# Two token chunks projected from raw activations, and the step sizes ahead of the last values

## The chip, the cores and the metric

The kernel runs on one core of a Trainium2 chip. The metric is the device time of one execution in microseconds. A core has five engines that matter here: TensorE (matrix products into PSUM banks), VectorE, ScalarE and GpSimd (elementwise work), and SyncE, which with ScalarE issues the DMAs. Each engine takes its instructions in a fixed order.

## The reference

One decoder layer on 1024 tokens of 1024 channels, with 16 learned meta tokens in front (1040 tokens in all). What matters for the change is the beginning: a root-mean-square norm, a projection, and of its parts the stick-breaking attention's q, k and v and the SSM's raw step sizes.

```python
h = jnp.concatenate([pad, meta_tokens, x], axis=1)
hn = rmsnorm(h, mix_norm_g)            # x * rsqrt(mean(x*x) + 1e-6) * g, per token
proj = hn @ w_in
sb_q, sb_k, sb_v, ssm_z, ssm_xbc, ssm_dt, c_q, c_kv, k_r = jnp.split(proj, split_at, axis=-1)
o_sb  = stick_breaking_attention(sb_q, sb_k, sb_v, valid)     # 8 heads of 64
dt = jax.nn.softplus(ssm_dt + dt_bias) * valid                # 16 heads
dA = dt * -exp(a_log); Acs = cumsum(dA within blocks of 128)  # used by the SSD stage later
...                                    # SSD, latent attention, output projection, SwiGLU, final norm
```

The norm's factor 1/rms is one number per token, so a projection can be made from `x * g` and multiplied by the token's factor afterwards.

## The kernel before

Channels lie on partitions and tokens along the free axis. Every fp32 operand is split into a high and a low fp32r part, and each product is three matmuls (high x high, low x high, high x low) that add into one PSUM bank. `dense_fm` makes one such product for a chunk of tokens: 8 slices of channels x 3 = 24 matmuls. The bank comes from `dpool`, which has two (`d_ps`), and is free again when its evacuation function has read it. `HH` and `HL` (`hnh`, `hnl` in the profile, one tile for each of 8 channel slices) hold the high and low parts of the activations.

The tokens come in three chunks (`CH_ALL`): chunk 0 of 272, chunks 1 and 2 of 384 columns. The first stage makes, for each chunk, the keys (`w_k`) and queries (`w_q`) of the first pair of heads and the values (`w_v`) of half the heads, the latter in three blocks of up to 128 tokens, 24 matmuls of 256 columns each.

- Chunk 0 goes *raw*: `first_operands(0)` splits `x * g`, and the evacuations multiply by the token factor. `k_evac` and `q_evac` do it with `over_rms` (one VectorE product into `scaled`), `sb_values` by ScalarE's `scale`. Later `normalise(0, row)` overwrites `HH` and `HL` of chunk 0 for the rest of the kernel.
- Chunks 1 and 2 are normalised before they are projected. `chunk_rstd` squares x on ScalarE, adds the eight slices up on VectorE (`acc`), sums over channels by a matmul with ones (`ssum`), takes the power -1/2 on GpSimd (`rc`), spreads the factor over partitions by three matmuls (`rrow`) and copies it out (`row`). `normalise` multiplies x by gain and row on VectorE (in place in `xT`), casts the high part on ScalarE and subtracts the low part on VectorE, for chunk 0 mostly on GpSimd.

After that come the values' loads (`load_value_steps`, through DRAM tensor `s_vsb`; `vlast` and `V` are what the attention reads), then `step_sizes`: a projection with 96 columns (`w_dt`), transposes into `dtt`, a softplus by polynomial in some 20 small VectorE instructions, a running sum by one matmul (`acum`, copied to `AT`), its transposes (`acst`), and a split of that sum into three bf16 rows (`A3`, through slices of the buffers `raws[2]` and `raws[3]`, 18 VectorE instructions). Then the attention of four pairs of heads begins. Score products (`sc_ps`), a sigmoid on ScalarE and a scan on VectorE (`cm`), transposes (`ptm`, `ptg`) and weighted values (`pv`) follow each other; the projections of the next pair and the convolution units (`conv_unit`) are put between them.

The order on each engine is set by a scheduler that places the instructions by its own time line as it builds the program; `tc.high_priority` moves evacuations and statistics forward. Tiles come from pools with a fixed number of buffers, and a tile that reuses a buffer waits for the last reader of the one before.

Of the kernel before, what the change touches and what calls it, by code (L numbers as in the profile page):

```python
# [11 lines left out]
F32 = mybir.dt.float32  # L12
# [8 lines left out]
D = 1024  # L21
KT = D // 128
# [37 lines left out]
def tile_hybrid_block(ctx: ExitStack, tc: tile.TileContext, a: dict):  # L60
# [5 lines left out]
    def last_on(engine):  # L66
        return next(i for i in reversed(nc.cur_bb.bb.instructions) if i.engine == engine)
# [71 lines left out]
    def dense_fm(dpool, w, nkt, m, mov, chunks, evac):  # L139
        hi, lo = w  # L140
        for c0, n in chunks:
            ps = dpool.tile([128, 512], F32, tag="d", name="d_ps")
            for kt in range(nkt):
                mh, ml = mov(kt, c0, n)
                wh = hi[:, kt * m : (kt + 1) * m]
                wl = lo[:, kt * m : (kt + 1) * m]
                pe.matmul(ps[:m, :n], wh, mh, start=(kt == 0), stop=False)  # L147
                pe.matmul(ps[:m, :n], wl, mh, start=False, stop=False)  # L148
                pe.matmul(ps[:m, :n], wh, ml, start=False, stop=(kt == nkt - 1))  # L149
            with tc.high_priority(offset=1000):  # L150
                evac(ps, c0, n)

    def token_rstd(cols, ps, squares, blocks, width, bufs=1):


        for e, (t0, w) in enumerate(blocks):
            for i, sq in enumerate(squares):
                pe.matmul(
                    ps[:w, e : e + 1], sq[:, t0 : t0 + w], ones[:, 0:1], start=(i == 0), stop=(i == len(squares) - 1)
                )  # L160
        nb = len(blocks)
        r = cols.tile([128, nb], F32, tag=f"rc{nb}", bufs=bufs, name="rc")
        e0 = 0
        if blocks[0][1] < 128:
            w = blocks[0][1]
            dve.memset(r[:, 0:1], 1.0)
            dve.tensor_scalar(r[:w, 0:1], ps[:w, 0:1], 1.0 / width, EPS, ALU.mult, ALU.add)
            e0 = 1
        dve.tensor_scalar(r[:, e0:nb], ps[:, e0:nb], 1.0 / width, EPS, ALU.mult, ALU.add)
        pool.tensor_tensor(r, r, mhalf[:, :nb], op=ALU.pow)  # L170
        return r
# [24 lines left out]
    def fill_tile(tag, name):  # L196
        return fl.tile([128, 388 if tag == "craw" else 384], F32, tag=tag, name=name)
# [44 lines left out]
    def chunk_rstd(i):  # L242
        c0, n = CH_ALL[i]
        blocks = [(t0 - c0, w) for t0, w in BLOCKS[3 * i : 3 * i + 3]]
        acc = fill_tile("cacc", "acc")[:, :n]
        for k in range(KT):
            x = xT[:, k, c0 : c0 + n]
            sq = acc if k == 0 else sqs[k % 2][:, 512 * (k // 2 % 2) :][:, :n]
            act.activation(sq, x, AF.Square)
            if k > 0:  # L250
                dve.tensor_tensor(acc, acc, sq, op=ALU.add)
        ssum = ps0.tile([128, 4], F32, tag="ssum", name="ssum")
        with tc.high_priority(offset=200):
            r = token_rstd(p0, ssum, [acc], blocks, D, bufs=3)
            rrow = ps0.tile([128, 512], F32, tag="rrow", bufs=1, name="rrow")
            spread(rrow, r, blocks, 0)
            row = fill_tile("craw", "row")
            act.copy(row[:, :n], rrow[:, :n])
        return r, row

    def normalise(i, row):
        c0, n = CH_ALL[i]
        c = slice(c0, c0 + n)
        for k in range(KT):
            hn = xT[:, k, c]
            dve.scalar_tensor_tensor(hn, hn, gmix[:, k : k + 1], row[:, :n], ALU.mult, ALU.mult)
            act.copy(HH[k][:, c], hn)
            eng = pool if i == 0 and k not in (2, 5, 7) else dve
            eng.tensor_tensor(HL[k][:, c], hn, f32(HH[k][:, c]), op=ALU.subtract)
# [338 lines left out]
        return (Q, K, KS), k_evac, q_evac  # L608


    proj, k_evac, q_evac = sb_project(0)

    def first_pair(name):
# [7 lines left out]
    stats = [chunk_rstd(0)]  # L621
# [17 lines left out]
    sp.dma_start(acol, a["a_log"].partition_broadcast(128))  # L639
    for i, (q0, qn) in enumerate(((0, 256), (256, 384), (640, 384))):  # L640
        c0, n = CH_ALL[i]
        if i < 2:
            r1, row1 = chunk_rstd(i + 1)
            normalise(i + 1, row1)
        if i == 0:
            r, row = stats[0]
            dense_fm(dpool, w_k, KT, 128, hn_mov, [(c0, n)], lambda ps, t0, m: k_evac(ps, t0, m, row[:, :m]))
            t1 = META + q0 - c0
            dense_fm(dpool, w_q, KT, 128, hn_real, [(q0, qn)], lambda ps, t0, m: q_evac(ps, t0, m, row[:, t1 : t1 + m]))
            sb_values(0, w_v, range(3), r, ps0)  # L650
        else:
            dense_fm(dpool, w_k, KT, 128, hn_mov, [(c0, n)], k_evac)
            dense_fm(dpool, w_q, KT, 128, hn_real, [(q0, qn)], q_evac)
            sb_values(0, w_v, range(3 * i, 3 * i + 3), None, ps0)
    normalise(0, row)
    p0_st.close()

    with ctx_sb as st:
# [32 lines left out]
                    weighted_values(tp, pvp, sbb, j, rows, values[0], h, [x[p, 64 * h : 64 * (h + 1)] for x in (s_osbh, s_osbl)], pms[j % 2], values[1])  # L691

        values = load_value_steps(sbv, sbb, 0)
        step_sizes()
        convs = [8, 9, 10, 11, 0, 1, 2, 3, 4, 5, 6, 7]
        for p in range(4):
            sb_attend(p, proj, values)
# [1051 lines left out]
```

## Time and profile before

| | |
|---|---|
| median of 3 runs | 1794.79 us (1790.23 to 1795.47) |
| the profiled execution | 1792.69 us, its span 1791.0 us |
| mean granted TensorE clock | 0.978 |
| TensorE busy | 1714.3 us (96%), 9801 matmuls |
| VectorE busy | 1129.1 us (63%) |
| ScalarE busy | 842.9 us (47%) |
| GpSimd busy | 718.0 us (40%) |

The busy share is a mean over stages. The profile's slices show TensorE at nine tenths or more in nearly all of the span, and lower in the first 5%; a wait shows in brackets behind an instruction of the time line, with the engine and the tile that ended it. Line numbers are those of the kernel before.

### The profile page before, as it was taken

How to read it: one execution, taken by the hardware profiler on the slowest of the kernel's cores; microseconds unless marked ns; L12 is line 12 of the kernel's file. 1: busy time of each engine (PE TensorE's matmuls, PEld its weight loads, DVE VectorE, ACT ScalarE, POOL GpSimd, SP SyncE). 2: the span in 40 equal slices, each digit the busy share in tenths (PEclk: the TensorE clock that was granted, in tenths of full speed). 3: DMA queues.
4: the chain of work that ended last, by engine and by line, in shares of the span. 5: the costliest groups of instructions: out<-in, count | busy, mean ns of one | idle time of the engine just before them, and what ended most of it. 6: DMA issues, size and time to landing. Idle time of an engine off the chain costs nothing. (4 is left out here: it accounts for less than half of the span.)

```text
span 1791.0 us, 26537 instructions
## 1 busy us (share of the span) xinstructions
PE 1714.3 (96%) x9801; PEld 1505.6 (84%) x9801; DVE 1129.1 (63%) x1727; ACT 842.9 (47%) x1789; POOL 718.0 (40%) x503
## 2 busy tenths in 40 slices
PE   5969999999999998999999999999999999999998
PEld 5959998999988778998888887778888888878887
DVE  7476755777554564455675645887566666678654
ACT  6355555555566664677453433532222223244332
POOL 4232434434456556555321245554545555300002
PEclk8989999999999999999999998999999999999999
DMA  4221223222263455345531334122332322899702
GB/s 159 57 56 39 82 76 90 65 59 78 76 175 106 158 178 171 112 124 171 191 95 42 101 123 145 43 94 76 112 107 100 111 95 88 300 376 376 262 1 95
DMA packets 145639, 222.35 MB, mean 124 GB/s; under 512 B 24722, under 2 KB 84148, under 8 KB 145508
## 3 DMA queue, kind: packets, MB, share of 16 engines
q1 hardware_dynamic: 126112, 205.09, 35.2%
q10 hardware_dynamic: 19396, 15.56, 2.9%
q8 instruction: 77, 1.26, 0.3%
q14 instruction: 54, 0.44, 0.1%
HBM read 157.56 MB, written 63.04 MB: 123 GB/s over the span
## 5 line engine op out<-in xcount | busy, mean ns | idle before, releaser
L147 PE MATMUL d_ps<-hnh,whi 128*128 128x384 f32 (+6 forms) x744 | 247.7, 333 | 3.2 <-DVE KS L599 2.1
L149 PE MATMUL d_ps<-hnl,whi 128*128 128x384 f32 (+6 forms) x744 | 246.6, 331 | 0.0
L148 PE MATMUL d_ps<-hnh,wlo 128*128 128x384 f32 (+6 forms) x744 | 245.7, 330 | 0.0
L136 POOL TENSOR_TENSOR wlo<-wraw,whi 128x1024 fp32r<-128x1024 f32 (+1 forms) x57 | 138.6, 2432 | 191.8 <-ACT whi L134 190.4
L147 PEld LDWEIGHTS d_ps<-hnh,whi 128*128 128x128 f32 (+1 forms) x744 | 140.5, 189 | 8.0 <-DVE KS L599 2.5
L149 PEld LDWEIGHTS d_ps<-hnl,whi 128*128 128x128 f32 (+1 forms) x744 | 140.6, 189 | 3.3 <-issue 1.0
L148 PEld LDWEIGHTS d_ps<-hnh,wlo 128*128 128x128 f32 (+1 forms) x744 | 140.7, 189 | 2.3 <-issue 0.2
L1257 PE MATMUL b_ps<-T,wl 128*128 128x512 f32 x352 | 138.8, 394 | 1.3 <-POOL wl L1088 1.3
L1258 PE MATMUL b_ps<-T,wh 128*128 128x512 f32 x352 | 138.3, 394 | 1.3 <-DVE T L1088 1.3
L1256 PE MATMUL b_ps<-T,wh 128*128 128x512 f32 x352 | 139.0, 395 | 0.0
L308 DVE TENSOR_TENSOR pl<-ptg,ph 128x512 fp32r<-128x512 f32 (+1 forms) x160 | 99.4, 627 | 43.7 <-ACT ph L307 42.0
L1087 ACT CAST op<-raw 128x1024 fp32r<-128x1024 f32 x69 | 71.1, 1050 | 108.8 <-PE d_ps L1541 63.0
L679 DVE TENSOR_TENSOR_SCAN cm<-cm,zcol 128x144 f32<-128x144 f32 (+3 forms) x64 | 102.9, 1617 | 16.8 <-ACT cm L677 16.3
L1088 DVE TENSOR_TENSOR op<-raw,op 128x1024 fp32r<-128x1024 f32 x69 | 85.1, 1243 | 38.6 <-ACT op L1087 38.6
L307 ACT CAST ph<-ptg 128x512 fp32r<-128x512 f32 (+1 forms) x160 | 85.5, 541 | 32.0 <-PE ptg L324 21.4
L1088 POOL TENSOR_TENSOR wlo<-raw,whi 128x1024 fp32r<-128x1024 f32 x18 | 45.1, 2508 | 110.2 <-ACT whi L1087 110.2
L1088 POOL TENSOR_TENSOR wl<-raw,wh 128x512 fp32r<-128x512 f32 x46 | 74.3, 1623 | 29.8 <-ACT wh L1087 29.8
L491 DVE SCALAR_TENSOR_TENSOR cacc<-d_ps,cw,cacc 128x384 f32<-128x384 f32 (+3 forms) x108 | 61.8, 572 | 36.7 <-ACT cacc L484 34.7
L1087 ACT CAST wh<-raw 128x512 fp32r<-128x512 f32 x88 | 53.1, 615 | 65.8 <-PE b_ps L1258 65.8
L1094 POOL TENSOR_TENSOR tt<-tt 128x512 f32<-128x512 f32 (+1 forms) x8 | 8.1, 1011 | 187.0 <-ACT tt L1611 186.8
L1257 PEld LDWEIGHTS b_ps<-T,wl 128*128 128x128 f32 x352 | 66.4, 189 | 16.8 <-POOL wl L1088 1.6
L1258 PEld LDWEIGHTS b_ps<-T,wh 128*128 128x128 f32 x352 | 66.3, 188 | 16.7 <-DVE T L1088 1.6
(439 smaller groups left out, 5165.6 us busy)
## 6 DMA issues: line engine op xcount, KB each, us to landing
raw<-in_w_down_dram SPq DMA_DIRECT2D x99, 256.0 KB, 5.3
s_hops<-gs SPq DMA_DIRECT2D x63, 256.0 KB, 2.0
raw<-s_hops SPq DMA_DIRECT2D x63, 256.0 KB, 5.3
raw<-in_w_gate_dram SPq DMA_DIRECT2D x22, 512.0 KB, 3.5
raw<-in_w_up_dram SPq DMA_DIRECT2D x22, 512.0 KB, 3.9
wraw<-in_w_o_dram SPq DMA_DIRECT2D x16, 512.0 KB, 4.4
wraw<-in_w_xbc_dram SPq DMA_DIRECT2D x12, 512.0 KB, 3.6
s_xs<-csig SPq DMA_DIRECT2D x24, 192.0 KB, 2.5
```

The costliest lines, as they stand in the source:

```text
L136: pool.tensor_tensor(lo[:, :cols], raw[:, :cols], f32(hi[:, :cols]), op=ALU.subtract)
L147: pe.matmul(ps[:m, :n], wh, mh, start=(kt == 0), stop=False)
L148: pe.matmul(ps[:m, :n], wl, mh, start=False, stop=False)
L149: pe.matmul(ps[:m, :n], wh, ml, start=False, stop=(kt == nkt - 1))
L307: act.copy(ph[:, :n], pt[:, :n])
L308: dve.tensor_tensor(pl[:, :n], pt[:, :n], f32(ph[:, :n]), op=ALU.subtract)
L679: dve.tensor_tensor_scan(rev, rev, zcol.to_broadcast([128, n_all]), 1.0, ALU.mult, ALU.add)
L1087: act.copy(hi, value)
L1088: eng.tensor_tensor(lo, value, f32(hi), op=ALU.subtract)
L1256: pe.matmul(banks[j], hi[:, ks], UH[u][k], start=start and k == 0, stop=False, skip_group_check=skip)
L1257: pe.matmul(banks[j], lo[:, ks], UH[u][k], start=False, stop=False, skip_group_check=skip)
L1258: pe.matmul(banks[j], hi[:, ks], UL[u][k], start=False, stop=stop and k == 3, skip_group_check=skip)
```

## The change

Chunk 1 is projected raw as well: `first_operands(1)` comes ahead of its statistics, and its keys, queries and values are multiplied by the token factor when they are evacuated. Only chunk 2 is normalised before it is projected. For chunk 2 the eight squares are not added up on VectorE; they stay in the halves of the four `raws` buffers, and TensorE sums them in 24 matmuls with ones instead of three. Chunks 0 and 1 are normalised after chunk 2, behind the products that read them raw (`issue_after(normal)`). `step_sizes` is called before the values of the last chunk instead of after the value loads. `row` has a buffer of its own.

```diff
 def chunk_rstd(i):
-        acc = fill_tile("cacc", "acc")[:, :n]
+        if i == 2:
+            squares = [raws[k // 2][:, 512 * (k % 2) :][:, :n] for k in range(KT)]
+        else:
+            acc = fill_tile("cacc", "acc")[:, :n]
+            squares = [acc]
         for k in range(KT):
             x = xT[:, k, c0 : c0 + n]
-            sq = acc if k == 0 else sqs[k % 2][:, 512 * (k // 2 % 2) :][:, :n]
+            if i == 2:
+                sq = squares[k]
+            else:
+                sq = acc if k == 0 else sqs[k % 2][:, 512 * (k // 2 % 2) :][:, :n]
             act.activation(sq, x, AF.Square)
-            if k > 0:
+            if i < 2 and k > 0:
                 dve.tensor_tensor(acc, acc, sq, op=ALU.add)
...
-            r = token_rstd(p0, ssum, [acc], blocks, D, bufs=3)
+            r = token_rstd(p0, ssum, squares, blocks, D, bufs=3)
...
-            row = fill_tile("craw", "row")
+            row = p0.tile([128, 384], F32, tag="row", bufs=3, name="row")
...
     for i, (q0, qn) in enumerate(((0, 256), (256, 384), (640, 384))):
         c0, n = CH_ALL[i]
+        if i == 0:
+            first_operands(1)
+            stats += [chunk_rstd(1), chunk_rstd(2)]
         if i < 2:
-            r1, row1 = chunk_rstd(i + 1)
-            normalise(i + 1, row1)
-        if i == 0:
-            r, row = stats[0]
+            r, row = stats[i]
...
-            sb_values(0, w_v, range(3), r, ps0)
+            if i == 0:
+                normalise(2, stats[2][1])
+                normal = last_on(DVE)
+            sb_values(0, w_v, range(3 * i, 3 * i + 3), r, ps0)
         else:
             dense_fm(dpool, w_k, KT, 128, hn_mov, [(c0, n)], k_evac)
             dense_fm(dpool, w_q, KT, 128, hn_real, [(q0, qn)], q_evac)
+            with tc.issue_after(normal):
+                for e in range(2):
+                    normalise(e, stats[e][1])
+            step_sizes()
             sb_values(0, w_v, range(3 * i, 3 * i + 3), None, ps0)
-    normalise(0, row)
...
         values = load_value_steps(sbv, sbb, 0)
-        step_sizes()
```

The line numbers below are each kernel's own; a line of before past 660 stands seven to fourteen lines further down in the changed kernel.

VectorE ahead of chunk 1's column sums, where chunk 0's statistics (`rc`) have just been made. Before:

```order
L169 TENSOR_SCALAR rc<-ssum 128x2
L251 TENSOR_TENSOR acc<-acc,sqs 128x384 x7
L589 TENSOR_TENSOR scaled<-d_ps,row 128x272
L266 SCALAR_TENSOR_TENSOR xT<-xT,gmix,row 128x272 x8
L452 TENSOR_SCALAR acol<-acol 128x16
```

With the change:

```order
L169 TENSOR_SCALAR rc<-ssum 128x2
L240 SCALAR_TENSOR_TENSOR hnl_139<-xT,gmix,hnh_131 128x384
L240 SCALAR_TENSOR_TENSOR hnl_140<-xT,gmix,hnh_132 128x384
L258 TENSOR_TENSOR acc<-acc,sqs 128x384
...
L240 SCALAR_TENSOR_TENSOR hnl_146<-xT,gmix,hnh_138 128x384
L258 TENSOR_TENSOR acc<-acc,sqs 128x384 x2
L596 TENSOR_TENSOR scaled<-d_ps,row 128x272
```

Eight low parts of chunk 1 are put between its seven additions, and the multiplications of chunk 0 (`xT`, 272 columns) are gone from this place.

VectorE ahead of the step sizes, between chunk 2's normalisation and `dx`. Before:

```order
L269 TENSOR_TENSOR hnl_145<-xT,hnh_137 128x384
L269 TENSOR_TENSOR hnl_146<-xT,hnh_138 128x384
L598 TENSOR_TENSOR K<-d_ps,K 64x384
L599 TENSOR_TENSOR KS<-d_ps,K 64x384
L598 TENSOR_TENSOR K<-d_ps,K 64x384
L599 TENSOR_TENSOR KS<-d_ps,K 64x384
L606 TENSOR_TENSOR Q<-d_ps,Q 64x384 x2
L434 MEMSET dx 128x16
```

With the change:

```order
L273 SCALAR_TENSOR_TENSOR xT<-xT,gmix,row 128x384 x7
L276 TENSOR_TENSOR hnl_141<-xT,hnh_133 128x272
L273 SCALAR_TENSOR_TENSOR xT<-xT,gmix,row 128x384
L276 TENSOR_TENSOR hnl_144<-xT,hnh_136 128x272
L605 TENSOR_TENSOR K<-d_ps,K 64x384
L606 TENSOR_TENSOR KS<-d_ps,K 64x384
...
L276 TENSOR_TENSOR hnl_145<-xT,hnh_137 128x384
L276 TENSOR_TENSOR hnl_146<-xT,hnh_138 128x384
L605 TENSOR_TENSOR K<-d_ps,K 64x384
L606 TENSOR_TENSOR KS<-d_ps,K 64x384
L613 TENSOR_TENSOR Q<-d_ps,Q 64x384
L441 MEMSET dx 128x16
```

The second half of chunk 2's key evacuation stands behind the last low part of chunk 1.

TensorE around the running sum (`acum`). Before:

```order
L148 MATMUL d_ps<-hnh_138,wlo 128x384
L149 MATMUL d_ps<-hnl_146,whi 128x384
L456 MATMUL acum<-d_990,tri 128x144
L465 MATMUL acst<-identr,AT 16x16
L465 MATMUL acst<-identr,AT 16x128 x8
L312 MATMUL ptm<-identr,cm 16x128
```

With the change:

```order
L148 MATMUL d_ps<-hnh_138,wlo 128x384
L149 MATMUL d_ps<-hnl_146,whi 128x384
L463 MATMUL acum<-d_894,tri 128x144
L472 MATMUL acst<-identr,AT 16x16
L472 MATMUL acst<-identr,AT 16x128 x8
L575 MATMUL v_ps<-wv,hnh_131 128x256
...
L577 MATMUL v_ps<-wv,hnh_138 128x256
L685 MATMUL sc_ps<-K,Q 128x144
```

The last value block stands behind the running sum, and the first score product behind both; before, 22 score matmuls stood ahead of `acum`.

VectorE and ScalarE behind it: in the change the 18 instructions of the split stand directly behind the copy to `AT`, then the eight key evacuations of pair 1's first two chunks, then the first scan; before, three scans stood ahead of `dx`, and the split stood among scans and evacuations. On ScalarE the table load ahead of `Exp` in `step_sizes` is gone. Before:

```order
L438 ACTIVATE d_990<-dx 128x144
L439 ACT_TABLE_LOAD
L439 ACTIVATE d_990<-d_990 128x144
L677 ACT_TABLE_LOAD
```

With the change:

```order
L445 ACTIVATE d_894<-dx 128x144
L446 ACTIVATE d_894<-d_894 128x144
L474 COPY raw<-acst 16x272
```

The first sigmoid, with the one table load, stands behind pair 1's key casts.

## The prediction, made before the result was known

> **What bounds the kernel now.** I read the stages first (busy time in chosen stretches), then TensorE's rows in order of time with the waits in brackets, then the engines those waits name. Over the whole span TensorE is busy 96%, so time is to be had only where it stands still or runs at a low granted clock. Outside the end of the program that is in three stretches, all before 142 us:
>
> ```profile
> 24.00:48.00 24.00, 13.50 (x73) 12.64 (x74) 22.24 (x45) 14.57 (x35) 5.42 (x6) 0.72 0.04 12
> 100.00:115.50 15.50, 5.37 (x26) 3.29 (x25) 10.71 (x21) 5.75 (x11) 4.41 (x4) 0.80 0.11 34
> 115.50:142.00 26.50, 19.76 (x94) 17.11 (x93) 22.22 (x38) 13.09 (x32) 2.89 (x2) 0.73 0.05 11
> ```
>
> Columns: stretch, length, busy of TensorE, weight loads, VectorE, ScalarE, GpSimd, granted clock. TensorE stands for 10.5, 10.1 and 6.7 us, and VectorE is nearly full in the first and the third. The waits themselves:
>
> ```profile
> 24.91 0.80 PE L158 MATMUL ssum<-ones,acc 128*128 128x1 f32 x6 [1.35 <-DVE acc L251]
> 33.07 0.93 PE L176 MATMUL rrow<-identr,rc 128*128 128x128 f32 x6 [3.35 <-POOL rc L170]
> 38.44 0.69 PE L147 MATMUL d_ps<-hnh,wk 128*128 128x384 f32 x1 [4.44 <-ACT hnh L267]
> 39.25 0.52 PE L147 MATMUL d_ps<-hnh,wq 128*128 128x384 f32 x1
> 39.57 0.52 PE L148 MATMUL d_ps<-hnh,wq 128*128 128x384 f32 x1
> 42.54 0.69 PE L149 MATMUL d_ps<-hnl,wk 128*128 128x384 f32 x1 [1.81 <-DVE hnl L269]
> ...
> 102.99 0.45 PE L671 MATMUL sc_ps<-K,Q 128*128 128x400 f32 x1 [2.21 <-ACT cm L677]
> 112.32 0.85 PE L456 MATMUL acum<-d,tri 128*128 128x144 f32 x2 [7.52 <-DVE d L454]
> 115.48 0.38 PE L312 MATMUL ptm<-identr,cm 128*16 128x128 f32 x1
> ```
>
> The first stretch is chunk 1 (384 columns) waiting for its normalisation. The second is the step sizes: `acum` waits 7.5 us for VectorE's polynomial. The third is the start of attention. Until 47.8 the 384-wide matmuls follow each other at 0.32 us; at full clock the spacings are these (20 intervals, 57 matmuls, three column sums, the whole step-size projection):
>
> ```profile
> 48.27:51.79 3.52, 3.52 (x21) 3.36 (x20) 0.00 (x0) 0.49 (x2) 1.00 0.00 0
> 72.50:79.28 6.78, 6.73 (x57) 6.75 (x57) 0.74 (x2) 1.00 0.38 116
> 51.79 0.72 PE L158 MATMUL ssum<-ones,acc 128*128 128x1 f32 x6
> 52.38 0.42 PE L147 MATMUL d_ps<-hnh,wq 128*128 128x384 f32 x1
> 79.28 0.29 PE L147 MATMUL d_ps<-hnh,whi 128*96 128x272 f32 x1
> ...
> 91.25 0.41 PE L149 MATMUL d_ps<-hnl,whi 128*96 128x384 f32 x1
> ```
>
> So 0.176 us for a 384-wide matmul, 0.118 for a 256-wide one, 0.20 for one column sum (0.59 / 3), 12.4 for the step-size projection.
>
> **The change, step by step,** on before's clock.
>
> *A. Chunk 1 raw.* Its low parts and its seven additions, 15 vector instructions instead of 7, now stand between 15.7 us and the column sums, under GpSimd's weight subtractions:
>
> ```profile
> 16.05 6.07 DVE L251 TENSOR_TENSOR acc<-acc,sqs 128x384 f32<-128x384 f32 x3 [1.41 <-ACT sqs L249]
> 19.27 2.43 POOL L231 TENSOR_TENSOR wv<-raw,wv 128x1024 fp32r<-128x1024 f32 x1
> 22.21 1.22 DVE L251 TENSOR_TENSOR acc<-acc,sqs 128x384 f32<-128x384 f32 x2
> ```
>
> Three additions took 6.07 us while GpSimd worked, then 0.61 each. If again three get through by 22.1, the other twelve at 0.54 end at 28.6. TensorE, without the 1.35 us wait, gets to the sums at about 26.0 and waits 2.6. After the sums and ten leftover value matmuls (1.2) chunk 1's first key matmul runs at 30.5 instead of 38.44, and its low parts are long there.
>
> *B. Chunk 1 and 2 on TensorE.* 24 key matmuls (4.2), 24 column sums of chunk 2 instead of 3 (4.8, so 4.2 more than before), two spreads (1.3), 24 query (4.2), 72 value (8.5): 53.5. Then keys, queries and two value blocks of chunk 2 (4.2 + 4.2 + 5.7): 67.6. Chunk 2's sums stand after 14 of chunk 1's key matmuls and end at about 38.4.
>
> *C. What is late next.* The step-size projection needs a `d_ps` bank, and the two banks hold chunk 2's keys and queries. The last half of the keys is taken out on VectorE behind the whole normalisation of chunks 0 and 1, and all of it behind chunk 2's:
>
> ```profile
> 26.39 4.40 DVE L266 SCALAR_TENSOR_TENSOR xT<-xT,gmix,row 128x272 f32<-128x272 f32 x8
> 28.87 1.93 DVE L266 SCALAR_TENSOR_TENSOR xT<-xT,gmix,row 128x272 f32<-128x272 f32 x2
> 41.94 3.36 DVE L269 TENSOR_TENSOR hnl<-xT,hnh 128x384 fp32r<-128x384 f32 x7
> 52.28 0.55 DVE L598 TENSOR_TENSOR K<-d_ps,K 64x384 fp32r<-64x384 f32 x1 [3.66 <-ACT KS L597]
> 58.09 4.32 DVE L266 SCALAR_TENSOR_TENSOR xT<-xT,gmix,row 128x384 f32<-128x384 f32 x8 [0.85 <-ACT row L258]
> 26.00:48.00 22.00, 5.58 (x11) 4.32 (x5) 0.69 0.04 13
> 73.13 1.83 POOL L136 TENSOR_TENSOR wlo<-wraw,whi 128x768 fp32r<-128x768 f32 x1
> ```
>
> Before's sums of chunk 2 end at 52.38 and its normalisation begins at 58.09, 5.7 later; so here it begins at 44.1. From there: chunk 2 4.3 + 3.8 (in time for TensorE, at 52.2 against 53.5), chunk 0 4.4 + 1.3, chunk 1 4.3 + 3.8, eight evacuations at 0.55: 26.3, so 70.4. GpSimd meanwhile does five subtractions of chunk 0 (4.32 in the row 26.00:48.00, which counts line 269 alone, VectorE first, GpSimd second) and two weight halves (1.83 and, as in the row of A, 2.43). With GpSimd at work two vector instructions took 1.93 where eight took 4.40. If each of the seven only adds half a microsecond, the bank is free at 73; if each holds one vector instruction for its whole length, 8.6 less the seven instructions' own 3.5, at 75.5; at the other end, 70.4. I take 73, the row at 28.87 being the same pair of operations under the same work. TensorE waits 5.4 us, and I add 2 us of low clock, from the stretch after 38.44 (9.4 us, of which 3.4 lost after two waits). The projection ends at 73 + 12.4 + 2 = 87.4. Before has it at 91.7 with a value block more (24 x 0.118 = 2.8), so 1.5 us are left of the gain.
>
> The Trainium skill, "GPSIMD Engine Reference", Specifications, says that GpSimd shares its SBUF interfaces with VectorE and contends with vector instructions that have two SBUF inputs. By that the evacuations, which read a bank and one SBUF tile, would not be held, and the multiplications and subtractions would: nearer 75.5 than 70.4. Before's additions, three in 6.07 us, agree.
>
> *D. Step sizes ahead.* After the projection come pair 1's first two key chunks, already before the wait (24 x 272, 24 x 384 and transposes, 7.6 us): 95.0. The chain beside it:
>
> ```profile
> 99.63 1.28 ACT L439 ACT_TABLE_LOAD   x1
> 101.28 0.24 DVE L442 TENSOR_SCALAR d<-d 128x144 f32<-128x144 f32 x1 [2.02 <-ACT d L439]
> 103.44 1.32 DVE L679 TENSOR_TENSOR_SCAN cm<-cm,zcol 128x528 f32<-128x528 f32 x1 [0.84 <-ACT cm L677]
> 104.69 1.30 DVE L444 TENSOR_TENSOR d<-d,d 128x144 f32<-128x144 f32 x1
> 106.02 0.31 DVE L445 TENSOR_TENSOR d<-d 128x144 f32<-128x144 f32 x1
> 110.92 1.34 DVE L454 TENSOR_TENSOR d<-DT,acol 128x144 f32<-128x144 f32 x1
> 114.50:130.00 15.50, 0.00 (x0) 0.00 (x0) 6.74 (x18) 1.13 (x3) 0.00 (x0) 0.72 0.03 6
> ```
>
> From 101.28 to 112.26 it took 11.0: less the scan and its wait (2.2), less three instructions held to 1.3 each where a like one takes 0.31 (3.0), 5.8. Transposes done 90.8, copies and two ScalarE steps 1.1 (no score activation has run yet, so the table load between them should be gone), then 5.8: `acum` at 97.7, up to 102.0 if load and holds stay. TensorE waits 2.7. With `AT` and `acst` (2.0 of the 3.2 between the rows at 112.32 and 115.48, which ran at low clock), the moved value block (2.8) and nine score matmuls (1.2) it is at 103.7.
>
> *E. The split of the running sum,* 18 vector instructions, 6.74 us (the last row, which counts the tile `raw` alone), now stands ahead of pair 1's key evacuation: from 99 to 105.8, and six evacuations of about 0.5 to 108.7. TensorE waits for that bank from 103.7: 5.0 us and, as above, some low clock (1.5). 19 key matmuls (3.4) and five score matmuls with their scan (1.0) then bring it to the first `ptm` at 114.6, against 115.5. It is 19 matmuls ahead (3.3) and eight score matmuls behind (1.0): a gain of 3.2 us.
>
> *F. The start of attention.* From 115.5 to 142 before loses 6.7 us standing and 19.76 x 0.27 = 5.3 to the clock. VectorE enters it without the split and without eight key evacuations, about 10 us lighter, and TensorE has projection matmuls between the scores. The gain lies between 0 and 12; I take 6.5.
>
> The copies of `row`, the eight casts of chunk 1 on ScalarE (15.1 to 28, where VectorE is the later) and two more `scaled` products (in C) cost nothing of their own.
>
> **Sum.** 3.2 + 6.5 = 9.7 us, against the profiled execution's 1792.7 (its span 1791.0): 1783. That execution lies 2.1 us below the median of the runs, 1794.79, and within their spread. From 142 on TensorE is the bound and the gain should stay, though small moves in the order reach much further, for which I allow 2 us either way.
>
> **The rivals.**
> *More.* C ends at 70, 3 us earlier, and F is filled wholly: 3.2 + 3 + 12, some 18 us, 1775. For it: GpSimd's five subtractions can lie beside instructions that wait anyway. Against it: the split is gone from F but its work is not.
> *The stall only moves.* C at 75.5 (2.5 later), the chain with its load and holds (4.3), and only 2 from F: 3.2 - 2.5 - 4.3 + 2, so 1.6 us over the profiled execution, 1794; the case as a whole reaches from 1789 to 1800. For it: every microsecond that VectorE is late in C to E goes straight to TensorE, and 22.2 of 26.5 us busy in F speak for little slack. Against it: GpSimd has little to do while the chain runs. The Trainium skill's rule on the shared interfaces, quoted in C, belongs to this case.
> *Slower: the last values come late.* Their copy on ScalarE now waits behind pair 1's key casts, and these behind the split, whose buffers the keys take over. From there:
>
> ```profile
> s_vsb<-vs ACTq DMA_DIRECT2D x5, 128.0 KB, 1.7
> 82.62 2.89 SPq L399 DMA_DIRECT2D vlast<-s_vsb  x4
> vst<-s_vsb SPq DMA_DIRECT2D x4, 8.0 KB, 2.1
> ```
>
> Copy at 108.3, store 2.0, four issues 2.9, two loads 2.9, GpSimd's difference 1.3: the cast into `V` at 117.5, and in ScalarE's order it stands ahead of later score activations. TensorE has two banks of projections to go on with, to about 122. Each microsecond of the cast beyond that is lost; slower by over 5.4 needs it at 137, and 1804 for instance at 142. Against it: 20 us of slack.
>
> **Chances.** About 0.3% (5.4 us) is what a measurement here can tell from no change. The forecast (1779 to 1787) 0.47, more 0.20, the moved stall 0.20, slower 0.13. Faster by over 0.3%: 0.67; within: 0.20; slower: 0.13. Range 1772 to 1796: F filled and C early at one end, C late with F empty at the other.
>
> **What would show it.** Chunk 1's first 384-wide `wk` matmul near 30 with no wait over 3 us ahead (A); 24 sums taking about 5 us (B); the first 96-column matmul waiting about 5 us for VectorE's `KS` near 73 (C); no table load before Exp and `acum` waiting under 4 us (D); a wait of about 5 us before pair 1's third key chunk (E); 115 to 142 above 24 us busy at clock 0.9 (F). Wrong if the 96-column matmuls start after 78 or ScalarE waits for `vst` past 122.

## The result: slower by 0.7%, and the profile after

The changed kernel took 1805.87 us (median of 4 runs, 1802.34 to 1808.49) against 1794.44 beside it: a ratio of 1.0067, 95% interval 1.0042 to 1.0092. The forecast was 1783. The profiled execution of the changed kernel took 1802.34 us, its span 1800.6. Times below are medians of all executions of a kernel; the ratios leave out one slow execution each of *before_held* (2701.56 us) and *two_places* (5799.85 us).

The stages first, in the columns of the prediction's rows:

```profile
24.00:48.00 24.00, 24.00 (x173) 23.63 (x172) 11.14 (x26) 10.75 (x27) 1.95 (x2) 0.93 0.04 13
100.00:115.50 15.50, 7.64 (x45) 6.48 (x44) 12.70 (x33) 5.53 (x15) 2.43 (x4) 0.89 0.02 5
115.50:142.00 26.50, 23.86 (x116) 21.17 (x117) 17.91 (x22) 15.32 (x35) 12.25 (x9) 0.87 0.41 92
```

TensorE has no idle time left between 24 and 48 us. Its rows up to 152 us show where it stands instead:

```profile
32.00 0.33 PE L147 MATMUL d_ps<-hnh,wk 128*128 128x384 f32 x1
36.02 4.52 PE L158 MATMUL ssum<-ones,raw 128*128 128x1 f32 x40
78.76 0.51 PE L147 MATMUL d_ps<-hnh,whi 128*96 128x272 f32 x1 [8.33 <-DVE KS L606]
102.92 0.51 PE L463 MATMUL acum<-d,tri 128*128 128x144 f32 x2 [2.79 <-DVE d L461]
116.42 0.69 PE L147 MATMUL d_ps<-hnh,whi 128*128 128x384 f32 x1 [5.46 <-DVE KS L606]
123.19 0.27 PE L319 MATMUL ptm<-identr,cm 128*16 128x128 f32 x1
137.42 0.39 PE L323 MATMUL pv<-pm,V 128*128 128x256 f32 x1 [1.61 <-DVE pm L322]
152.15 0.41 PE L147 MATMUL d_ps<-hnh,whi 128*128 128x388 f32 x1 [2.75 <-DVE Q L613]
```

These are the waits that the prediction named: for the bank of the step sizes, for `acum`, for pair 1's keys. TensorE also stands longer than in the kernel before at a place a thousand microseconds later, where the residual stream is added up ahead of the last stage. TensorE, VectorE and GpSimd of the changed kernel there:

```profile
1067.38 0.50 PE L1370 MATMUL d_ps<-raw,whi 128*128 128x512 f32 x1 [2.75 <-DVE hT L1079]
1105.43 3.06 PE L158 MATMUL d_ps<-ones,sq 128*128 128x1 f32 x26 [0.97 <-ACT sq L1383]
1117.98 2.08 PE L176 MATMUL d_ps<-identr,rc 128*128 128x128 f32 x8 [5.04 <-POOL rc L170]
1060.55 0.69 DVE L1079 TENSOR_TENSOR hT<-hT,d_ps 128x512 f32<-128x512 f32 x1 [2.03 <-PE d_ps L149]
1061.15 4.97 DVE L1189 TENSOR_TENSOR rraw<-rraw,grow 128x512 f32<-128x512 f32 x2
1066.65 0.67 DVE L1079 TENSOR_TENSOR hT<-hT,d_ps 128x512 f32<-128x512 f32 x1
1060.37 2.42 POOL L136 TENSOR_TENSOR wlo<-wraw,whi 128x1024 fp32r<-128x1024 f32 x1 [4.84 <-ACT whi L134]
1062.75 2.83 POOL L1101 TENSOR_TENSOR raw<-xraw,raw 128x1024 fp32r<-128x1024 f32 x1
1114.17 2.34 POOL L136 TENSOR_TENSOR wlo<-wraw,whi 128x1024 fp32r<-128x1024 f32 x1 [3.98 <-ACT whi L134]
1116.47 1.47 POOL L170 TENSOR_TENSOR rc<-rc,mhalf 128x4 f32<-128x4 f32 x1
```

The same places in the kernel before (its lines are 13 less):

```profile
1099.26 6.23 PE L158 MATMUL d_ps<-ones,sq 128*128 128x1 f32 x28 [3.05 <-ACT sq L1370]
1110.13 1.05 PE L176 MATMUL d_ps<-identr,rc 128*128 128x128 f32 x8
1057.54 1.67 DVE L1176 TENSOR_TENSOR rraw<-rraw,grow 128x512 f32<-128x512 f32 x1
1059.30 0.69 DVE L1066 TENSOR_TENSOR hT<-hT,d_ps 128x512 f32<-128x512 f32 x1
1061.73 0.69 DVE L1176 TENSOR_TENSOR rraw<-rraw,grow 128x512 f32<-128x512 f32 x1 [1.75 <-DMA rraw<-s_omla]
1105.77 1.02 POOL L170 TENSOR_TENSOR rc<-rc,mhalf 128x4 f32<-128x4 f32 x1 [1.58 <-DVE rc L169]
1106.76 2.37 POOL L136 TENSOR_TENSOR wlo<-wraw,whi 128x1024 fp32r<-128x1024 f32 x1
```

The work is the same, and the change touches none of it. But `hT`, which frees a bank, now stands behind both `rraw` products instead of between them, and `rc` behind the `wlo` that it stood ahead of. An engine goes through its queue in order. So `rc` starts only when `wlo` is done, and that waits 3.98 us for ScalarE. The two `rraw` products wait for nothing in the changed kernel, but they are long: 2.18 and 2.86 us (4.97 together), each beside a GpSimd instruction of 2.42 or 2.83 us, where the second one took 0.69 in the kernel before, behind a wait of 1.75 us for its DMA. `hT` starts only when they are done. TensorE waits 8.8 us at these three rows, 3.05 before.

To see where time is won and lost over the span I laid traces over each other by TensorE's work: every matmul counts at a price of its form that is the same for all kernels (column sums left out), and the figure is by how many microseconds a kernel is later than the kernel before when it has done the same amount. It is of one profiled execution each, and single executions lie up to 7 us from their median (that of *two_places* is 7.0 below it):

```
before's clock at        75    145    300    560   1060   1200
changed kernel         -6.2   -9.6   -2.2   +3.8   +4.0   +9.1
before_held            +0.5  -10.9   -7.5   -2.6   -1.6   +3.1
after_held1            -6.1   -9.2    0.0   -0.1   -2.7   -4.1
steps_back             -6.3   -1.7   -5.5   -5.5  -13.3  -15.1
before_sb              +0.8   -2.2   -4.7   -4.8   -9.4  -10.5
vector_sums_same_order -14.0  -15.9  -11.0   -6.5   -5.7   -4.2
two_places             -7.6  -10.8   -4.5   +0.3   -0.3   -8.0
```

The column at 145 depends on the price. If each form counts at the usual distance from one such matmul to the next in the kernel before, the changed kernel is only 6.2 ahead there, *before_held* 9.2, *after_held1* 6.0, *vector_sums_same_order* 14.1 and *two_places* 7.2; the other columns move by 0.3 at most.

At 145 us the changed kernel was 9.6 ahead, as forecast (9.7), or 6.2 by the second price. It then gave back 7.4 by 300 (about 4 by the second price), 6.0 more by 560 and 5.1 between 1060 and 1200. So some 4 of the 9.1 us that it is behind at 1200 were there by 560, and 5 came at the place shown.

### The profile page after: what moved, and what is told of

Read it like the earlier page. It is cut to its first block, busy times and chain, and to the rows that moved or that the text cites. A ratio compares the mean times of both kernels' runs of the same rounds, so it can differ in the third digit from the quotient of the medians.

```text
span 1800.6 us, 26643 instructions
## 1 busy us (share of the span) xinstructions
PE 1721.6 (96%) x9843; PEld 1511.5 (84%) x9843; DVE 1144.4 (64%) x1730; ACT 842.2 (47%) x1795; POOL 718.5 (40%) x503
## 5 line engine op out<-in xcount | busy, mean ns | idle before, releaser
L693 DVE TENSOR_TENSOR_SCAN cm<-cm,zcol 128x144 f32<-128x144 f32 (+3 forms) x64 | 112.5, 1764 | 18.8 <-ACT cm L691 18.4
L1104 DVE TENSOR_TENSOR raw<-raw 128x512 f32<-128x512 f32 x58 | 58.9, 1022 | 44.2 <-DMA raw<-in_w_gate_dram 38.5
L134 ACT CAST whi<-wraw 128x1024 fp32r<-128x1024 f32 (+1 forms) x57 | 58.9, 1034 | 57.3 <-PE d_ps L149 26.9
```

What stands on the lines that cost most here:

```text
L693: dve.tensor_tensor_scan(rev, rev, zcol.to_broadcast([128, n_all]), 1.0, ALU.mult, ALU.add)
```

## The experiments

Two theories: *head* (Theory 1), that what the head gains or owes decides, whatever order comes behind; *order* (Theory 2), that the head keeps its gain and the scheduler's other order of the same later work loses it. Each kernel ran beside the kernel before; ratios are to that.

**The head under another order.** In these kernels the instructions traced from a mark on are chained on each engine in the order that another kernel has there. The edges set the order of issue and add no wait.

```diff
+        tc.held_from = len(nc.cur_bb.bb.instructions)   # where attention begins
         convs = [8, 9, 10, 11, 0, 1, 2, 3, 4, 5, 6, 7]
...
+    for name, steps in ORDER:             # per engine, the other kernel's order
+        own = [i for i in traced if i.engine.name == name]
+        at = np.cumsum(steps) - 1
+        for k, j in zip(at, at[1:]):
+            tc.add_manual_dep(own[j], own[k].name, no_sync, reason="held order")
```

*after_held*, the changed head with before's order from attention on:

> The changed kernel, but from the start of attention on every engine takes its instructions in the order that the kernel before has there (order edges alone, no waits added; the 48 key matmuls of pair 1 that stood ahead of the running sum therefore stand behind the first scores again). Theory 1, given back: the 9.6 us that TensorE was ahead at 145 us were paid with work that attention needs later as filling, since pair 0's scores, scans and transposes start some 13 us later behind step sizes, last values and split; whatever the order, that comes back, so 1795 to 1803. Theory 2, redrawn order: the head's gain is real, and it is lost because the scheduler drew another order of the same work from attention to 1100 us. Then the gain stays: 1783 as forecast, and up to 4 more because acum loses the cover of 24 key matmuls (4.2 us): 1783 to 1788.

1805.23, ratio 1.0062 (1.0042 to 1.0083), above the ranges of both theories. Not the test that it was meant to be: with none of pair 1's key matmuls ahead of it, `acum` was waited for 7.3 us, and further waits made the head itself 17.2 us late at 145. From there on it lost nothing more and got 5 us back (12.1 at 1200). So before's order lost nothing more here, behind a late head.

*before_held*, the old head in the changed order:

> The converse: the kernel before, with the changed kernel's order from the start of attention on. Theory 1: the later order is the one that suits a late start of attention and costs little by itself: 1790 to 1798. Theory 2: that order is what costs about 19 us (9.6 gained by 145, 9.3 behind at the end), so the kernel before gets slower by most of it: 1803 to 1813, a few us less since 73 key matmuls now cover the wait for acum (7.5 us before).

1796.83, ratio 1.0013 (0.9999 to 1.0026). By its time it speaks for *head* (1790 to 1798) and against *order*; its trace says something else. With none of the change in its head it is 10.9 us ahead at 145 (9.2 by the second price), and it gives that lead and 3 us more back by 1200. That order takes 48 of pair 1's key matmuls ahead of the first score product and 19 more ahead of the first `ptm`; in the kernel before the scores start with none of them done. So this lead at 145 is work moved forward, not time saved.

*after_held1*, the changed kernel in its own order through pair 0, then before's (the mark ahead of pair 1's attention):

> The changed kernel in its own order through pair 0's attention, and from pair 1's attention on in the order of the kernel before. Theory 1, head: the start of attention is late and TensorE's lead is owed, so the loss stays: 1800 to 1806. Theory 2, order: the 6 us lost between 350 and 520 us and the 5 us between 1040 and 1160 us go with the order that lost them, while those at 145-215 us stay: 1793 to 1798.

1792.37, ratio 0.9987 (0.9971 to 1.0003): 13.5 us under the changed kernel with the same head. That is just below *order*'s 1793 to 1798, and *head* falls. The trace shows it level with the kernel before at 300.

*after_ssd_order*, the mark ahead of the SSD stage:

> The changed kernel in its own order through all four pairs of attention, and from the SSD stage (about 560 us) on in the order of the kernel before. By the traces the changed kernel loses some 6 us between 430 and 520 us and some 6 between 1020 and 1120 us. Theory places: each is lost by the order at its own place, so the second goes: 1797 to 1801. Theory chain: they are one debt, TensorE being ahead of what it should have kept, and what isn't lost there is lost elsewhere: 1803 to 1808.

1796.54, ratio 1.0010 (0.9995 to 1.0026), just below *places* (1797 to 1801), and *chain* falls. Holding only what lies behind 560 us takes away 9 of the 11 us.

**Orders alone.** *steps_back* has the call of `step_sizes` at its old place and the rest of the change:

```diff
-            step_sizes()
             sb_values(0, w_v, range(3 * i, 3 * i + 3), None, ps0)
...
         values = load_value_steps(sbv, sbb, 0)
+        step_sizes()
```

> Only the raw chunk 1 and the sums on TensorE: the step sizes stand behind the value loads as before. TensorE keeps the 6 us that the changed kernel was ahead between 50 and 75 us, the 8.3 us wait for the step-size projection's bank has a value block more in front (4.2 us), and the polynomial's 7.5 us wait ahead of acum is back. Theory 1: attention is not behind the step sizes, so the head's gain stays: 1787 to 1791. Theory 2: about 1794 plus or minus 8, as the order is drawn anew.

1782.33, ratio 0.9931 (0.9913 to 0.9950), the fastest so far and below both ranges. *Head* seemed proved. But its lead at 145 is 1.7 us, so two kernels were run across: its head in before's order, and before's head in its order.

> Raw chunk 1 and sums on TensorE, step sizes at their old place (the kernel that ran at 1782.3), but from the start of attention on in the order of the kernel before. Both stand in the same order up to the first weighted values anyway, and there TensorE was only 1.7 us ahead of the kernel before. Theory 1, head: what the raw chunk saves is real and stays: 1779 to 1785. Theory 2, order: of its 11 us only the 1.7 are the head's, the others were gained at 215-350, 520-720 and 1040-1160 us by the order drawn: 1790 to 1793.

1788.33, ratio 0.9964 (0.9947 to 0.9981): 6 us are left, between the two theories.

> The converse: the kernel before, computing what it computes, with the order of the kernel that ran at 1782.3 from the start of attention on. Theory 1, head: 1791 to 1796. Theory 2, order: 1781 to 1787, faster than the kernel before without any part of the change.

1783.33, ratio 0.9935 (0.9912 to 0.9957), as *order* said. The kernel before gains 11 us without any part of the change, from the order alone. The same order behind the changed head (from pair 1 on):

> The changed kernel in its own order through pair 0's attention, and from pair 1's attention on in the order of the kernel with the step sizes back (1782.3). The kernel before took 1783.3 in that order, which gained 9 us between 220 us and the end. Theory order: the changed kernel in before's order from pair 1 on took 1792.4, and here 9 us less: 1781 to 1787. Rival: orders pay only with the head that they were drawn for: 1790 to 1798.

1791.36, ratio 0.9967 (0.9955 to 0.9980). A miss for *order*: of 9 us it kept one against after_held1. Its trace is 6.5 us later between 200 and 210 us, where the two orders meet.

**Does any new order move the time?** Two kernels with before's head and work:

```diff
-            with tc.high_priority(offset=1000):
+            with tc.high_priority(offset=950):
                 evac(ps, c0, n)
```

> The kernel before with one number changed that is no work: the evacuations of projections are put forward by 950 places instead of 1000. The order is the same up to 559 us and drawn anew from there to 1087 us. Theory 1, head: nothing in the head differs, 1791 to 1796. Theory 2, order: the same work in another order ends 3 to 8 us away from 1793.4, on either side.

1794.48, ratio 0.9995 (0.9980 to 1.0010). And one with four copies made twice:

```diff
             act.copy(ph[:, :n], pt[:, :n])
+            if len(pv_first) < 4:
+                pv_first.append(act.copy(ph[:, :n], pt[:, :n]))
```

> The kernel before with the first four copies of transposed weights in pair 0's attention made twice on ScalarE (about 2 us of its time, none of TensorE's, the same result): the order is the same up to 120 us and drawn anew from there. Theory any order: a fresh order is good for 5 us or more either way, as it was for the change (1805.9 against 1792.4) and for the step sizes back (1783.3 against 1794.4): below 1789 or above 1799. Theory pulled forward: only an order that moves pair 1's projections ahead of the first scores loses, 1791 to 1798 here.

1793.18, ratio 0.9999 (0.9985 to 1.0012). Not in these two: here an order drawn anew is worth nothing that can be told from zero, while particular orders above lose or win 10 us. Two draws do not say how often either happens.

**The parts.** *late_split* moves the split of the running sum behind pair 0's attention (its three rows in `craw` tiles):

```diff
         for p in range(4):
             sb_attend(p, proj, values)
...
+            if p == 0:
+                split_running_sum()
             for u in convs[3 * p : 3 * p + 3]:
```

> The changed kernel with the split of the running sum (18 vector instructions, 6.7 us, eight transposes and three copies) behind pair 0's attention instead of directly behind the running sum; its result is needed only some 450 us later. Theory 1: the wait for pair 1's third key chunk (5.5 us at 116) goes, attention starts about 7 us earlier, and that stays: 1796 to 1800. Theory 2: what is gained at 116 is within what any redrawn order gives or takes later; the time may end anywhere from 1794 to 1810, and the lag at 145 us will not tell where.

1793.73, ratio 0.9997 (0.9983 to 1.0011), just below both ranges. Its trace is 22.9 us ahead at 145 (20 by the second price) and 6.6 behind at 300. Part of this lead was only lent: the moved split stands between 183 and 197 us, and in the stretch from 170 to 215 us TensorE stands 8.4 us and runs at clock 0.85, where the kernel before does not stand at all.

The next three keep the changed kernel's order from attention on and differ in the head; with the changed kernel (1805.87) and before_held (1796.83) they share all that follows.

> Raw chunk 1 and sums on TensorE, step sizes at their old place, but from the start of attention on in the changed kernel's order. With the changed kernel (1805.9) and the kernel before in that order (1796.8) it is one of four kernels that differ in the head alone. Theory S: in this order the 9 us between those two are the cost of the early step sizes, and the raw chunk saves 1 to 6 us: 1790 to 1796. Theory R: they are the cost of the raw chunk and its 24 sums, whose gain at 50 us is paid at 79: 1800 to 1806.

1802.71, ratio 1.0032 (1.0016 to 1.0049).

> The fourth of these heads: chunk 1 normalised first and its sums as before, only the step sizes (with chunk 0's normalisation, which they need) ahead of the last values; the changed kernel's order from the start of attention on. Theory S: 1800 to 1806. Theory R: 1793 to 1798.

1796.90, ratio 1.0012 (0.9997 to 1.0027). So in this order theory S falls: the early step sizes cost nothing (1796.90 against 1796.83), and the raw chunk with its 24 sums costs 5.9 us (1802.71 against 1796.83) to 9.0 (1805.87 against 1796.90); by the ratios, each to the kernel before beside it, 3.4 to 9.9.

*vector_sums_same_order* adds chunk 2's squares up on VectorE:

```diff
-        if i == 2:
-            squares = [raws[k // 2][:, 512 * (k % 2) :][:, :n] for k in range(KT)]
-        else:
-            acc = fill_tile("cacc", "acc")[:, :n]
-            squares = [acc]
+        acc = fill_tile("cacc", "acc")[:, :n]
+        squares = [acc]
```

> The changed kernel with chunk 2's squares added up on VectorE, so three column sums instead of 24 (4.2 us less on TensorE) and seven additions more on VectorE (about 4 us); the changed kernel's order from attention on. The 24 sums lie ahead of the 8.3 us wait for the bank, whose end is set by VectorE, so what they cost on TensorE is hidden in that wait and the additions make it longer: 1804 to 1809. Rival: the sums are on the path and 4 us are saved: 1800 to 1803.

1796.06, ratio 0.9996 (0.9984 to 1.0008): 9.8 us less, more than either theory allowed, so in this order the 24 sums are all that the raw chunk costs. Part of the reason shows in one row:

```profile
73.12 0.51 PE L147 MATMUL d_ps<-hnh,whi 128*96 128x272 f32 x1 [10.54 <-DVE KS L606]
```

The step sizes start at 73.12 instead of 78.76. The sums are not hidden in the wait for the bank; they put its end off (below, C).

> The changed kernel with chunk 2's squares added up on VectorE, in its own order all the way (its 19 scores then stand ahead of pair 1's other projections). In the changed kernel's order it took 1796.1. Theory sums: the 24 sums cost about 10 us, so 1793 to 1799 here too. Theory order: its own order decides, and it ends more than 4 us from 1796.

1793.78, ratio 0.9999 (0.9987 to 1.0010), in the range of *sums* and as in the changed order. With the step sizes at their old place, in the order of steps_back:

> Raw chunk 1 alone: step sizes at their old place and chunk 2's squares added up on VectorE, from attention on in the order in which the kernel with the 24 sums took 1782.3. Theory sums: what the 24 sums cost on the way to the bank of the step sizes (6 us by the traces) is saved here too: 1773 to 1779. Rival: in this order the polynomial's wait ahead of acum takes it back: 1780 to 1785.

1781.55, ratio 0.9930 (0.9916 to 0.9945), level with steps_back and in the rival's range, but not for the rival's reason: behind `acum`, at 145, its trace is still 4.6 us ahead of that one, and the lead has shrunk to 1.4 only by 560.

**The two places.** The changed order with only these neighbours exchanged:

```diff
 DVE
-L1189 TENSOR_TENSOR rraw<-rraw,grow 128x512 x2
-L1101 TENSOR_TENSOR rows<-rraw,rows 128x512
+L1189 TENSOR_TENSOR rraw<-rraw,grow 128x512
 L1079 TENSOR_TENSOR hT_11266<-hT_11266,d_ps 128x512
-L1101 TENSOR_TENSOR rows<-rraw,rows 128x512
+L1189 TENSOR_TENSOR rraw<-rraw,grow 128x512
+L1101 TENSOR_TENSOR rows<-rraw,rows 128x512 x2
 POOL
-L136 TENSOR_TENSOR wlo<-wraw,whi 128x1024
 L170 TENSOR_TENSOR rc<-rc,mhalf 128x4
+L136 TENSOR_TENSOR wlo<-wraw,whi 128x1024
```

> The changed kernel in its own order but for two neighbours. On VectorE, near 1061 us, the evacuation of a bank (hT) stands ahead of the second product with the row sums (rraw), which waits for a DMA; in the changed kernel it stands behind, and TensorE waits 2.75 us for the bank at 1067. On GpSimd, near 1114 us, the power for the row sums (rc) stands ahead of a weight half (wlo), which waits 4 us for ScalarE; in the changed kernel it stands behind, and TensorE waits 5.04 us for it at 1118. Both as in the kernel before. Theory places: the two waits and the low clock behind them are what the order loses there, less about 3 us that the kernel before waits for its last squares: 1798 to 1801. Theory chain: TensorE waits elsewhere for the same time: 1803 to 1808.

1793.45, ratio 0.9992 (0.9977 to 1.0007), below both ranges: the two exchanges are worth 12.4 us. That is more than the changed kernel loses here: in the table it falls back 5.1 us between 1060 and 1200, where this kernel gains 7.7 on the kernel before. So the exchanges make good the loss of this place and, as a gain over the kernel before, most of the rest. The expectation that `rraw` waits for a DMA did not hold in either kernel; here the two products take 2.25 and 2.27 us, and `hT` between them 0.68.

TensorE in its trace, where the waits stood:

```profile
1061.48 0.50 PE L1372 MATMUL d_ps<-raw,whi 128*128 128x512 f32 x1 [0.62 <-POOL raw L1101]
1096.56 3.06 PE L158 MATMUL d_ps<-ones,sq 128*128 128x1 f32 x26
1103.68 1.27 PE L176 MATMUL d_ps<-identr,rc 128*128 128x128 f32 x8
```

And 1040 to 1180 us of the kernel before, the changed one and this, in this order:

```profile
1040.00:1180.00 140.00, 133.94 (x597) 110.10 (x597) 94.72 (x125) 54.27 (x90) 72.03 (x43) 0.94 0.31 100
```

```profile
1040.00:1180.00 140.00, 129.19 (x576) 105.31 (x575) 90.00 (x114) 53.17 (x87) 71.97 (x43) 0.93 0.32 103
```

```profile
1040.00:1180.00 140.00, 135.90 (x628) 110.48 (x627) 101.65 (x132) 56.58 (x93) 73.53 (x44) 0.99 0.32 108
```

From the changed kernel to this one the idle time falls by 6.7 us and the granted clock rises from 0.93 to 0.99, by an estimate 8 us more over 136 busy microseconds (136 x 0.06). The windows do not hold quite the same work, and the table has 12.8 for both together. Not even the 3.05 us wait of the kernel before is left. The same exchange under the head with VectorE's sums:

> The same two exchanges in the changed kernel with chunk 2's squares added up on VectorE, which in its own order took 1793.8 and waits 3.48 and 3.02 us at these two places. Theory places: 1787 to 1791. Theory chain: 1792 to 1796.

1784.97, ratio 0.9952 (0.9934 to 0.9971): 9 us under vector_sums, below the range of *places* and again more than the waits alone. It and, at 1782 to 1783, steps_back, back_vector_sums and before_sb beat both kernels by some 10 us; steps_back_held and after_other_order do so by less.

## Why the prediction was wrong

**A held**, 1.5 us late. Chunk 1's first 384-wide matmul ran at 32.00 (30.5 forecast), with no wait ahead of it. **B held as a price**: 20 of chunk 2's sums took 4.52 us (the row counts 40 matmuls), 0.23 each. They ended at 40.5, where the prediction had 38.4.

**C was mis-sized**, 8.33 us for 5.4, the bank free at 78.6 for 73; the first 96-column matmul at 78.76 is past the 78 that the prediction had set against itself. VectorE in the changed kernel:

```profile
40.58 0.16 DVE L169 TENSOR_SCALAR rc<-ssum 128x3 f32<-128x3 f32 x1 [6.46 <-PE ssum L158]
43.91 0.56 DVE L596 TENSOR_TENSOR scaled<-d_ps,row 128x384 f32<-128x384 f32 x1 [3.16 <-PE d_ps L149]
47.33 4.33 DVE L273 SCALAR_TENSOR_TENSOR xT<-xT,gmix,row 128x384 f32<-128x384 f32 x8
60.87 7.26 DVE L273 SCALAR_TENSOR_TENSOR xT<-xT,gmix,row 128x272 f32<-128x272 f32 x8
70.42 5.39 DVE L276 TENSOR_TENSOR hnl<-xT,hnh 128x272 fp32r<-128x272 f32 x7
```

I let the normalisation of chunk 2 begin 5.7 us behind its sums, at 44.1. It began at 47.33: the sums were 2 us late, VectorE stood 6.46 us for them and then 3.16 for chunk 1's first keys, which TensorE could finish only behind the 24 sums, and their evacuation stands first in VectorE's queue. That is what vector_sums_same_order takes away. The rest is time beside GpSimd. Eight multiplications took 7.26 us, 0.91 each against 0.54 in the row at 47.33, and unevenly: the longest took 2.20. Of the seven subtractions one took 2.70 and the others about 0.5. GpSimd meanwhile did this:

```profile
57.71 5.76 POOL L276 TENSOR_TENSOR hnl<-xT,hnh 128x272 fp32r<-128x272 f32 x5 [16.04 <-ACT hnh L274]
63.44 2.16 POOL L136 TENSOR_TENSOR wlo<-wraw,whi 128x768 fp32r<-128x768 f32 x1
70.64 2.41 POOL L136 TENSOR_TENSOR wlo<-wraw,whi 128x1024 fp32r<-128x1024 f32 x1 [5.04 <-ACT whi L134]
```

The Trainium skill, "GPSIMD Engine Reference", Specifications, says that vector instructions with two SBUF inputs contend with GpSimd; the trace agrees (2.70 us beside the weight half of 2.41, 2.20 beside that of 2.16), and `hT`, which reads a bank and one SBUF tile, took its usual 0.69 beside GpSimd at 1060.55. So the end that the prediction drew from it, 75.5, was nearer than 70.4, but still too low. GpSimd worked 10.3 us in these three rows, not the 8.6 reckoned with, and the late start stands on top. The reading of the rows for the unheld price was off as well: the two products at 28.87 are among the eight at 26.39, so the other six took 0.41 each, and the 4.4 us that stand in the sum already held about 1.1 us of such time.

**D and E held in the length of their waits**: 2.79 us for `acum` (2.7), no table load ahead of `Exp`, 5.46 us ahead of pair 1's third key chunk (5.0). Their places slipped, by 5.2 us at `acum` (102.92 for 97.7), of which C's 5.6 is the cause, by 7.7 at the key chunk (116.42 for 108.7) and by 8.6 at the first `ptm` (123.19 for 114.6). **F came just short of its sign** (above 24 us at 0.9): 23.86 us busy at clock 0.87. What that window loses falls from 12.0 us to 5.7 (2.6 standing and 3.1 by the clock), 6.3 less for a forecast of 6.5.

That the lead at 145 agrees with the sum is partly luck. By the table's way of counting TensorE was some 4 us behind the kernel before at 115.5, where the sum has it 3.2 ahead; from there to 142 it then gained 13 us on the same work, for 6.5. The two misses cancel.

**The step that failed** is the one behind the sum: "From 142 on TensorE is the bound and the gain should stay, though small moves in the order reach much further, for which I allow 2 us either way." It failed twice. First, the gain did not stay. The 9.7 us were counted as TensorE's lead, and the lead is there, but before_held has one of the same size with the old head: it is pair 1's projections, done early. That they are then missing as filling is my reading; no run tests it alone. Between 145 and 300 us TensorE stands 6.3 us in the changed kernel and 4.0 in the kernel before. When only the part through pair 0 runs in the changed order, 0.0 of the lead is left at 300, and the whole change is worth about 2 us, not to be told from none (after_held1, ratio 0.9971 to 1.0003). Second, 2 us for the order was too little by a factor of six: with the same head, the changed kernel's later order costs 13.5 us against before's (1805.87 and 1792.37), and two exchanges a thousand microseconds on are worth 12.4.

**The rivals.** *The stall only moves* comes nearest for the head: it was given 1794, and after_held1 took 1792.4. That is its number, not its terms: no table load came, and the start of attention gave more than the 2 us that it was allowed. *Slower: the last values come late* named a real delay. The sign that was set against the forecast appeared (ScalarE waits for `vst` at 126.28), and the last cast into `V` ran at 137.91, past its threshold:

```profile
126.28 0.62 ACT L363 CAST V<-vst 128x512 fp32r<-128x512 f32 x1 [1.58 <-POOL vst L417]
137.91 0.62 ACT L363 CAST V<-vst 128x512 fp32r<-128x512 f32 x1 [0.55 <-ACT oTs L357]
```

It was not the cause: TensorE has no wait for `V` there, and the early step sizes, which delay it, cost nothing in steps_only_same_order. No rival had the order as its mechanism.

**Open.** The two exchanges were not run apart. Nor do they say why the changed kernel loses 11 us and other heads in the same order do not: TensorE waits 6.7 us at the same three rows in before_held, 6.3 in steps_only_same_order and 6.5 in vector_sums_same_order, which are 9 to 10 us faster. Of that the wait for `rc` is 1.4 to 1.5 us in these three, and 5.0 and 4.2 in the two kernels of this order that have the 24 sums (the changed kernel and raw_only_same_order); why it depends on the head is not traced. By the heads the loss goes with the raw chunk and its 24 sums, by the exchanges with two neighbours in a queue; the two amounts overlap and do not add up. What the order of steps_back does better between 215 and 300 and between 560 and 1060 us, some 7 of before_sb's 10.5 us in the table, is not traced to instructions. That the sums cost 10 us in one order and one in another is measured, not explained.

## What to carry to other kernels

Work that an engine has done ahead is not time gained: ask whether it will be missed later as filling, and compare two kernels under the same later order before a lead is booked. Where a scheduler draws the order of a long program anew after every edit, compare the orders to the end and look in each queue for an instruction that waits or runs long and now stands ahead of one that TensorE waits for. A saving of a few microseconds in one stage cannot be judged from the total time while two exchanged pairs elsewhere are worth twelve.

## What was not expected of the hardware

A short wait can cost twice, by the granted clock behind it. In the changed kernel the stretch of the 2.75 us wait ran at 0.83 and that of the 5.04 us wait at 0.66. In two_places both stretches are at 1.00, though the second is other work there; its `rc` spread stands at 1103.68, and around that the clock was 0.86 with no wait of TensorE (columns: stretch, length, TensorE busy, granted clock, DMA share and GB/s; the changed kernel, then two_places):

```profile
1062.00:1072.00 10.00, 7.25 (x25) 0.83 0.21 63
1115.00:1125.00 10.00, 7.02 (x26) 0.66 0.02 8
```

```profile
1062.00:1072.00 10.00, 10.00 (x45) 1.00 0.54 202
1115.00:1125.00 10.00, 10.00 (x63) 1.00 0.07 28
1098.00:1110.00 12.00, 12.00 (x59) 0.86 0.32 89
```

The Trainium skill, "TensorE: Matmul & The Clock Gate", Why this matters for your kernels, asks for no gaps over about 3 us between bursts of matmuls; here the clock was low behind one of 2.75 us as well, and again in the 10 us behind the 2.75 us wait at 152.15 (0.83). How long a gap must be these runs do not settle: behind a 2.00 us wait for `ptm` near 850 us the next 10 us ran at 0.83 in the kernel before and at 1.00 in the changed kernel.
